# The opening rows of a decoder trunk: norm weights spread by TensorE, the root on ScalarE, two weight splits on GpSimd, orders fixed

## The chip, the cores and the metric

The kernel runs on one core of a Trainium2 chip. A core has five engines that run side by side: TensorE (PE in the profile, with its weight loads as PEld), VectorE (DVE), ScalarE (ACT), GpSimd (POOL) and SyncE (SP, which here only issues transfers). The metric is the device time of one execution in microseconds (us); lower is better.

## The reference

One layer of a decoder trunk on 1024 tokens of width 1024: a root-mean-square norm, eight input projections that feed two token mixers, an output projection, then a second norm and a squared-ReLU MLP, then a last norm. What matters here is the beginning:

```python
def rms_norm(x, gain):
    xf = x.astype(jnp.float32)
    y = xf * lax.rsqrt(jnp.mean(xf * xf, axis=-1, keepdims=True) + NORM_EPS)
    return (y * gain.astype(jnp.float32)).astype(x.dtype)
...
    h = rms_norm(x, norm_mix[l])
...
    proj = h @ w_in
    xa, ga, q, f, v, g, m_a, m_b = jnp.split(proj, SPLIT_POINTS, axis=-1)
```

## The kernel before, in words

The tokens are worked in two halves (c = 0 and 1) of 512, the width in four pairs (p) of 256 channels. All large products are made of three products of numbers in a shorter format: each float32 operand is split into a high part (H, a cast on ScalarE, L82) and a low part (L, the difference of the two, on VectorE, L83), and `mm3` (L119 to L123) multiplies H by L, H by H and L by H. Weights arrive as tiles of 128 x 1024 (`raw`, four buffers) and are split into `wH` and `wL` (six buffers, so three tiles at a time).

The opening is `first_norm(0)` followed by the first `project_v`. `first_norm(0)` issues, all on SyncE's queue, four blocks of 128 rows of x, the norm weights (`gain`, one row of 1024 that the transfer repeats on 128 partitions) and the first three weight tiles. `norm_rows` (L140) then takes a block's mean square (Square with an accumulator, ScalarE), adds epsilon (VectorE), raises to the power -0.5 (GpSimd), and scales the rows by that and by the gain in one VectorE instruction. `transposed` (L147) turns the block into columns by TensorE, in two halves of four 128 x 128 transposes (`xT`), and splits them into `hT0H` and `hT0L`. `project_v` makes `v` (`pv`, one PSUM bank per block of rows, accumulated over four weight tiles): with `by_rows` it takes the first three tiles block by block, then the fourth tile for all blocks. After it come the projections `xa` (`pj_xa`, whose first product ends the opening), `q` and `f`, the gate products `pr` and `pi` of the recurrence, and the rest of the first pair.

What sets the order: a scheduler places the instructions by its own estimate of their times. Only instructions that pass through `keep` while `in_order[0]` is true (that is, until the end of `first_norm(0)`) stay in the order in which the program states them; splits of weights carry a higher priority (`tc.high_priority(400)`). Each engine runs its own list strictly in order. The small tables `pvt`, `mf` and `mu` come on SyncE's queue behind the opening's transfers; `parameters` derives per-channel constants from `pvt` on VectorE and ScalarE.

Of the kernel before, what the change touches and what calls it, by code (L numbers as in the profile page):

```python
# [18 lines left out]
P = 128  # L19
# [23 lines left out]
def trunk(ctx: ExitStack, tc: tile.TileContext, x, wts, mlp, pv, gains, mask_f, mask_u, out):  # L43
# [15 lines left out]
    def bank(tag, name):  # L59
        return ps.tile([P, 512], F32, tag=tag, name=name, bufs={"pj": 4, "sc": 2, "hg": 2}[tag])  # L60
# [16 lines left out]
    def keep(ins):  # L77
        if in_order[0]:
            tc.keep_in_program_order(ins)

    def split(src, h, lo):
        keep(A.copy(h, src))  # L82
        keep(V.tensor_tensor(out=lo, in0=src, in1=h.bitcast(F32), op=ALU.subtract))  # L83

    def raw_tile(name):
        return wp.tile([P, 1024], F32, tag="raw", name=name, bufs=4)
# [1 line left out]
    def load_w(i):  # L88
        raw = raw_tile(f"raw{i}")
        nc.sync.dma_start(raw, wts[i])  # L90
        return raw

    def split_w(i, raw):
        h = wp.tile([P, 1024], F32R, tag="w", name=f"wH{i}", bufs=6)
        lo = wp.tile([P, 1024], F32R, tag="w", name=f"wL{i}", bufs=6)
        with tc.high_priority(400):
            split(raw, h, lo)
        return h, lo

    raws = []  # L100

    def fill_w(n):
        while made[0] < min(n, len(seq)):
            i = seq[made[0]]
            raw = raws.pop(0) if raws else load_w(i)
            ready[made[0]] = split_w(i, raw)
# [8 lines left out]
    def next_w():  # L115
        used[0] += 1
        return get_w(used[0] - 1)

    def mm3(o, ah, al, bh, bl, first, last, goes_on=False):  # L119
        how = {"skip_group_check": True} if goes_on else {}  # L120
# [2 lines left out]
        PE.matmul(o, al, bh, start=False, stop=last, **how)  # L123
# [7 lines left out]
    mhalf = const.tile([P, 8], F32, tag="mhalf", name="mhalf")  # L131
    G.memset(mhalf, -0.5)

    def gain_tile(i, queue=nc.scalar):
        g = const.tile([P, D], F32, tag="gain", name=f"gain{i}", bufs=1)
        queue.dma_start(g, gains[i : i + 1, :].to_broadcast([P, D]))
        return g


    def norm_rows(xt, xn, gain, name):  # L140
        r = const.tile([P, 1], F32, tag="rstd", name=f"rstd_{name}", bufs=4)
        keep(A.activation(xn, xt, AF.Square, scale=D**-0.5, accum_out=r))
        keep(V.tensor_scalar(r, r, EPS, None, op0=ALU.add))  # L143
        keep(G.tensor_tensor(out=r, in0=r, in1=mhalf[:, 0:1], op=ALU.pow))
        keep(V.scalar_tensor_tensor(xn, xt, r[:, 0:1], gain, op0=ALU.mult, op1=ALU.mult))

    def transposed(xn, dst, tt, name):  # L147
        for h in range(2):
            pt = bank("hg", f"xT_{name}_{h}")
            for k in range(4):  # L150
                PE.transpose(pt[:, k * P : (k + 1) * P], xn[:, (4 * h + k) * P : (4 * h + k + 1) * P], ident)
# [14 lines left out]
    def tile_x(name):  # L166
        return xt_pool.tile([P, D], F32, tag="xt", name=name)
# [8 lines left out]
    def mt(tag, name, shape=(P, T), dt=F32, bufs=1):  # L176
        return m.tile(list(shape), dt, tag=tag, name=name, bufs=bufs)
# [60 lines left out]

    X_TAGS = ("g1", "g2", "on", "xc")

    def first_norm(c):
        dst = a2_set(a2h, f"hT{c}")
        xts = []
        for tt in range(4):
            r = c * 4 + tt
            xt = mt(X_TAGS[tt], f"x{r}", (P, D)) if c == 0 else tile_x(f"x{r}")
            nc.sync.dma_start(xt, x[r * P : (r + 1) * P, :])
            xts.append(xt)
            if c == 0 and tt == 0:
                gain0.append(gain_tile(0, nc.sync))  # L250
            if c == 0 and tt < 3:
                raws.append(load_w(seq[tt]))
        xns = {}

        def rows(tt):
            xns[tt] = mt("f" if tt % 2 == 0 else "tmp", f"xn{c}{tt}", (P, D))
            norm_rows(xts[tt], xns[tt], gain0[0], f"x{c}{tt}")

        def weights(n):
            if c == 0:  # L260
                fill_w(n)

        rows(0)
        weights(1)
        transposed(xns[0], dst, 0, f"x{c}0")
        rows(1)
        weights(2)
        for tt in range(1, 4):
            if tt < 3:
                rows(tt + 1)  # L270
            transposed(xns[tt], dst, tt, f"x{c}{tt}")
        weights(3)
        in_order[0] = False
        hT.append(dst)

    def project(c, name):

# [10 lines left out]
    def project_v(c, name, by_rows):  # L288
        v = mt("v", f"v_{name}", (P, 4, 512))
        pp = [bank("pj", f"pv_{name}_{tt}") for tt in range(4)]  # L290
# [8 lines left out]
        early = 3 if by_rows else 0  # L299
        w = [next_w() for _ in range(early)]  # L300
        for tt in range(4):
            for j in range(early):
                product(tt, j, w[j])
        for j in range(early, V_TILES):
# [336 lines left out]

    for c in range(NC):
        if c == 0:
            first_norm(0)
            mu32 = small_inputs()
        else:
            out_proj(0, ys, res0, done0, lambda: first_norm(1))
        ys = a2_set(a2y, f"y{c}")
        for p in range(NPAIR):
            if p % 2 == 0:  # L650
                v = project_v(c, f"{c}{p}", c == 0 and p == 0)
# [417 lines left out]
```

## Time and profile before

| | |
|---|---|
| time, median of 3 runs | 1615.21 us (1615.21 to 1615.22) |
| profiled execution | 1614.85 us |
| its span on the core | 1613.1 us |
| granted TensorE clock, mean | 0.996 |
| busy: PE / DVE / ACT / POOL | 97% / 75% / 47% / 4% |
| first transposes start, first product, first product of pj_xa | 7.76, 10.06, 38.42 us |

Times in the profile are counted from the start of the span. In a row of the timeline stand start, duration, engine, line, operation, and what is written from what; in brackets the idle time of the engine before it and what ended that wait. In a row of waits stand the waiting instruction, the one that it waits for, the total, how often, and the longest. In a row of stretches stand the stretch, its length, then the busy time and the number of instructions of PE, PEld, DVE, ACT and POOL, the granted clock, the share of the transfer engines and GB/s. A row that names a line with three numbers between slashes gives the least, median and greatest duration in ns. A row of transfers ends in KB and in us from issue to landing.

### The profile page before, as it was taken

What the parts mean: (1) busy time and instruction counts of PE and PEld (TensorE: products, weight loads), DVE (VectorE), ACT (ScalarE), POOL (GpSimd) and SP (SyncE); (2) the same over time, 40 slices, a digit from 0 to 9 for tenths busy, and PEclk for the clock granted to TensorE, in tenths of its full rate; (3) what the DMA queues carried; (4) which work ended last, traced back from release to release, by engine and by line L of the source; (5) the groups of instructions that cost most, each with busy time, mean ns of one, the idle gap of its engine ahead of it and who ended that gap; (6) DMA issues with size and microseconds to landing.
All of it is one profiled execution on the core that took longest, in us unless ns stands there. A gap on an engine that the chain in (4) does not pass through costs nothing.

```text
span 1613.1 us, 22407 instructions
## 1 busy us (share of the span) xinstructions
PE 1567.8 (97%) x8856; PEld 1281.7 (79%) x8856; DVE 1209.2 (75%) x1751; ACT 760.2 (47%) x1170; POOL 63.7 (4%) x99
## 2 busy tenths in 40 slices
PE   7999999999999999999999997999999999999997
PEld 6878788787888878788787875888888878888886
DVE  4886954958762877856869688888887888888776
ACT  4544544445442644435444575766777732221113
POOL 0010100100100010000000000000000000000000
PEclk9999999999999999999999998999999999999999
DMA  6222222222244222223222363666666666666652
GB/s 239 92 71 94 86 79 91 81 79 97 80 163 143 93 66 92 79 84 100 67 92 92 118 209 105 248 245 257 242 243 256 223 256 239 256 243 256 247 206 105
DMA packets 57993, 246.46 MB, mean 153 GB/s; under 512 B 6688, under 2 KB 6816, under 8 KB 47136
## 3 DMA queue, kind: packets, MB, share of 16 engines
q1 hardware_dynamic: 56448, 239.79, 41.0%
q10 hardware_dynamic: 1440, 5.24, 1.0%
q8 instruction: 69, 1.13, 0.3%
q14 instruction: 36, 0.29, 0.1%
HBM read 185.24 MB, written 59.77 MB: 152 GB/s over the span
## 4 chain that ended last, share of the span: by engine, by line
PE 79%; DVE 16%; DMA 2%; issue 1%; ACT 1%; POOL 0%; SPq 0%; DVEq 0%; POOLq 0%; ACTq 0%
PE uX L121 3%; PE uX L123 3%; PE uX L122 3%; PE dX L121 3%; PE dX L122 3%; PE dX L123 3%; DVE wL L83 2%; PE pj_ga L123 2%; PE pj_ga L122 2%; PE pj_ga L121 2%; PE pj_ma L121 2%; PE pj_ma L123 2%; PE pj_ma L122 2%; PE pj_f L123 2%; PE pj_f L121 2%; PE pj_f L122 2%
## 5 line engine op out<-in xcount | busy, mean ns | idle before, releaser
L83 DVE TENSOR_TENSOR wL<-raw,wH 128x1024 fp32r<-128x1024 f32 x160 | 194.3, 1215 | 148.3 <-ACT wH L82 145.4
L82 ACT CAST wH<-raw 128x1024 fp32r<-128x1024 f32 x160 | 167.9, 1050 | 182.6 <-issue 51.8
L980 DVE TENSOR_TENSOR acc<-acc,dX 128x512 f32<-128x512 f32 x128 | 86.7, 682 | 27.6 <-PE dX L123 27.4
L82 ACT CAST wA<-q 128x512 fp32r<-128x512 f32 x32 | 19.8, 622 | 129.8 <-PE dX L123 81.9
L980 DVE TENSOR_TENSOR acc<-acc,dY 128x512 f32<-128x512 f32 x64 | 43.4, 683 | 13.8 <-PE dY L123 12.6
L361 DVE RECIPROCAL rr<-rr 128x512 f32<-128x512 f32 x16 | 53.5, 3346 | 0.0
L840 ACT ACTIVATE b<-b 128x512 f32<-128x512 f32 x48 | 30.2, 630 | 37.8 <-DVE b L839 37.8
L327 DVE SCALAR_TENSOR_TENSOR xc<-xp,pvt,xc 128x512 f32<-128x512 f32 x48 | 33.1, 745 | 0.0
L567 ACT ACTIVATE on<-po 128x128 f32<-128x128 f32 x64 | 16.9, 278 | 33.5 <-PE po L557 33.2
L586 ACT ACTIVATE smb<-pj_mb 128x512 f32<-128x512 f32 x16 | 9.6, 597 | 45.2 <-PE pj_mb L123 45.0
L841 ACT ACTIVATE b<-b 128x512 f32<-128x512 f32 x48 | 30.1, 630 | 1.1
L581 ACT ACTIVATE g<-pj_g 128x512 f32<-128x512 f32 x16 | 9.6, 599 | 37.3 <-PE pj_g L123 37.3
L400 DVE TENSOR_TENSOR seg<-seg 128x128 f32<-128x128 f32 (+2 forms) x96 | 26.9, 309 | 0.2
L460 POOL TENSOR_SCALAR seg<-seg 128x128 f32<-128x128 f32 (+1 forms) x16 | 12.6, 788 | 357.7 <-DVE seg L400 357.7
L123 PE MATMUL pj_ga<-hT1H,wL 128*128 128x512 f32 x64 | 26.5, 414 | 0.0
L121 PE MATMUL pv<-wL,hT0H 128*128 128x512 f32 x64 | 26.0, 406 | 0.3 <-DVE wL L83 0.3
L123 PE MATMUL pj_ga<-hT0H,wL 128*128 128x512 f32 x64 | 26.2, 409 | 0.0
L400 DVE TENSOR_TENSOR kk<-kk,seg 128x768 f32<-128x768 f32 (+1 forms) x32 | 26.1, 817 | 0.0
L122 PE MATMUL pj_ga<-hT0H,wH 128*128 128x512 f32 x64 | 25.8, 403 | 0.0
L121 PE MATMUL uX<-h2B11L,wA 128*128 128x512 f32 x64 | 25.0, 391 | 0.7 <-DVE rstd_h L143 0.7
L83 DVE TENSOR_TENSOR wA<-q,wA 128x512 fp32r<-128x512 f32 x32 | 21.9, 685 | 4.9 <-ACT wA L82 4.9
L123 PE MATMUL pv<-wH,hT0L 128*128 128x512 f32 x64 | 25.6, 400 | 0.0
(1854 smaller groups left out, 5167.0 us busy)
## 6 DMA issues: line engine op xcount, KB each, us to landing
raw<-wts_in SPq DMA_DIRECT2D x160, 512.0 KB, 3.3
q<-mlp_in SPq DMA_DIRECT2D x64, 512.0 KB, 3.6
x<-x_in SPq DMA_DIRECT2D x8, 512.0 KB, 6.1
acc<-x ACTq DMA_DIRECT2D x8, 512.0 KB, 5.4
y_out<-acc SPq DMA_DIRECT2D x16, 256.0 KB, 2.0
xs<-x_in SPq DMA_DIRECT2D x8, 256.0 KB, 3.9
x<-xs SPq DMA_DIRECT2D x8, 256.0 KB, 2.0
x2s<-x_in SPq DMA_DIRECT2D x4, 512.0 KB, 5.0
```

Of the source, the lines that this page charges most:

```text
L82: keep(A.copy(h, src))
L83: keep(V.tensor_tensor(out=lo, in0=src, in1=h.bitcast(F32), op=ALU.subtract))
L121: PE.matmul(o, ah, bl, start=first, stop=False, **how)
L122: PE.matmul(o, ah, bh, start=False, stop=False, **how)
L123: PE.matmul(o, al, bh, start=False, stop=last, **how)
L327: V.scalar_tensor_tensor(xc[:, s, :], xp[:, j : j + T], pvt[:, PV_CW + 8 * j + u : PV_CW + 8 * j + u + 1], xc[:, s, :], op0=ALU.mult, op1= ...
L361: V.reciprocal(rec, rec)
L400: mul = lambda o, a, b: V.tensor_tensor(out=o, in0=a, in1=b, op=ALU.mult)
L567: A.activation(on[:, 4 * s + n, :], po[:, n * P : (n + 1) * P], AF.Square, accum_out=ssq[:, 4 * s + n : 4 * s + n + 1])
L840: A.activation(b[:, at, :], b[:, at, :], AF.Relu, scale=-1.0 if at == 2 else 1.0)
L841: A.activation(b[:, at, :], b[:, at, :], AF.Square)
L980: V.tensor_tensor(out=dst, in0=dst, in1=banks[bk, pr], op=op)
```

## The change

The opening becomes a function of its own, `opening()`, and every instruction of it on TensorE, ScalarE, VectorE and GpSimd is kept in program order.

- The norm weights come as one row of 4 KB on ScalarE's queue. TensorE spreads them over the partitions by multiplying a column of ones with the row (two products of plain float32, 512 columns each) into two PSUM banks; VectorE reads them there, in two half-width scalings for each block. ScalarE copies them to SBUF later, for the second half of the tokens.
- Four products of a 128 x 128 tile of ones with itself stand on TensorE ahead of that, and four behind it. Their result is not used.
- The inverse root is Sqrt on ScalarE, with epsilon as its bias, and a reciprocal on VectorE; before, an addition on VectorE and a power on GpSimd. One Sqrt of a single column is run at the start, so the table that ScalarE loads is the one with Sqrt.
- The low parts of the first and the third weight tile are computed on GpSimd.
- SyncE's queue has x0, w0, x1, w1, w2, x2, x3; before it had x0, gain, w0, x1, w1, x2, w2, x3.
- The products of the first three weight tiles are stated block by block: for each tile first the products with its high part, those with its low part later (`product`), the transposes of the next block between them.

```diff
-    def split(src, h, lo):
+    def split(src, h, lo, engine=V):
         keep(A.copy(h, src))
-        keep(V.tensor_tensor(out=lo, in0=src, in1=h.bitcast(F32), op=ALU.subtract))
+        keep(engine.tensor_tensor(out=lo, in0=src, in1=h.bitcast(F32), op=ALU.subtract))
...
+    ones = const.tile([P, P], F32, tag="ones", name="ones")
+    V.memset(ones, 1.0)
+    unit = const.tile([P, 1], F32, tag="unit", name="unit")
+    A.activation(unit, ones[:, 0:1], AF.Sqrt)
...
-                PE.transpose(pt[:, k * P : (k + 1) * P], xn[:, (4 * h + k) * P : (4 * h + k + 1) * P], ident)
+                keep(PE.transpose(pt[:, k * P : (k + 1) * P], xn[:, (4 * h + k) * P : (4 * h + k + 1) * P], ident))
...
+    def opening():
+        dst = a2_set(a2h, "hT0")
+        hT.append(dst)
+        row = mt("seg", "g0row", (P, 1536))[0:1, 0:D]
+        nc.scalar.dma_start(row, gains[0:1, :])
+        xts = [mt(X_TAGS[tt], f"x{tt}", (P, D)) for tt in range(4)]
+        for what in ("x0", "w0", "x1", "w1", "w2", "x2", "x3"):
...
+        def pace(n):
+            for _ in range(n):
+                keep(PE.matmul(warm[:, 0:P], ones, ones, start=True, stop=True))
+
+        pace(4)
...
+        pg = [bank("sc", f"gain_ps{h}") for h in range(2)]
+        for h in range(2):
+            keep(PE.matmul(pg[h], ones[0:1, :], row[:, h * 512 : (h + 1) * 512], start=True, stop=True))
+        pace(4)
...
+        def stats(tt, whole=True):
...
+            keep(A.activation(xns[tt], xts[tt], AF.Square, scale=D**-0.5, accum_out=r))
+            keep(A.activation(r, r, AF.Sqrt, bias=eps_t))
+            if whole:
+                inverse(tt)
+
+        def scaled(tt):
+            for h in range(2):
+                xn, xt = xns[tt][:, halves[h]], xts[tt][:, halves[h]]
+                keep(V.scalar_tensor_tensor(xn, xt, rs[tt][:, 0:1], pg[h], op0=ALU.mult, op1=ALU.mult))
...
+        def product(tt, j, part):
+            for k in (2 * j, 2 * j + 1):
+                hh, hl = (a[:, tt * P : (tt + 1) * P] for a in kt(dst, k))
+                wh, wl = (a[:, k % 2 * 512 : (k % 2 + 1) * 512] for a in w[j])
+                for n, (a, b) in enumerate(((hh, wh), (hl, wh)) if part == "h" else ((hh, wl),)):
+                    keep(PE.matmul(pp[tt], a, b, start=(k, n, part) == (0, 0, "h"), stop=False))
+
+        stats(0)
+        scaled(0)
+        fill_w(1, G)
+        stats(1, False)
+        transposed(xns[0], dst, 0, "x00")
+        fill_w(2)
+        inverse(1)
+        scaled(1)
+        fill_w(3, G)
+        w.extend(next_w(False) for _ in range(3))
+        stats(2)
+        scaled(2)
+        for tt in range(4):
+            for j, part in ((0, "h"), (0, "l"), (1, "h"), (2, "h")):
+                product(tt, j, part)
+            if tt < 3:
+                transposed(xns[tt + 1], dst, tt + 1, f"x0{tt + 1}")
+            if tt == 0:
+                stats(3)
+                scaled(3)
+            for j in (1, 2):
+                product(tt, j, "l")
         in_order[0] = False
-        hT.append(dst)
+        for h in range(2):
+            A.copy(g[:, halves[h]], pg[h])
+        return pp
```

`project_v` then takes over the four banks (`begun`) and adds the fourth weight tile. Outside the opening the orders of the engines differ in the first pair of channels only.

The next rows are ScalarE's list from its first transfer or table load on, before. `xn` is a block's rows (the Square writes there, its sum goes to `rstd_x`), `wH` a weight tile's high part, `hT0H` the high part of a transposed half.

```order
L142 ACT_TABLE_LOAD
L142 ACTIVATE xn_126,rstd_x_127<-x_110 128x1024
L82 CAST wH_132<-raw_114 128x1024
L82 CAST hT0H_106<-xT_x_0_136 128x4x128
L82 CAST hT0H_107<-xT_x_1_143 128x4x128
L142 ACTIVATE xn_150,rstd_x_151<-x_116 128x1024
L82 CAST wH_156<-raw_118 128x1024
L142 ACTIVATE xn_160,rstd_x_161<-x_120 128x1024
```

And now:

```order
L267 DMA g0row<-gains_in 1x1024
L129 ACT_TABLE_LOAD
L129 ACTIVATE unit<-ones 128x1
L298 ACTIVATE xn_148,rstd_x_149<-x_116 128x1024
L299 ACTIVATE rstd_x_149<-rstd_x_149,eps_t 128x1
L82 CAST wH_155<-raw_121 128x1024
L298 ACTIVATE xn_159,rstd_x_160<-x_117 128x1024
L299 ACTIVATE rstd_x_160<-rstd_x_160,eps_t 128x1
L82 CAST hT0H_110<-xT_x_0_163 128x4x128
L82 CAST hT0H_111<-xT_x_1_170 128x4x128
L82 CAST wH_177<-raw_124 128x1024
L82 CAST wH_184<-raw_126 128x1024
```

The Square of the second block now stands ahead of the casts of the first block's transposed halves; the casts of the second and third weight tile stand together right behind them.

TensorE's list up to the first use of the second weight tile, before (`xT` are the transposes, `pv_0` the products of the first block):

```order
L151 MATMUL xT_x_0_136<-ident,xn_126 128x128 x4
L151 MATMUL xT_x_1_143<-ident,xn_126 128x128 x4
L121 MATMUL pv_0_227<-wL_133,hT0H_106 128x512
L122 MATMUL pv_0_227<-wH_132,hT0H_106 128x512
L123 MATMUL pv_0_227<-wH_132,hT0L_108 128x512
```

And now (`warm` takes the products of ones, `gain_ps` the spread norm weights):

```order
L280 MATMUL warm<-ones 128x128 x4
L287 MATMUL gain_ps_136<-g0row,ones 128x512
L287 MATMUL gain_ps_137<-g0row,ones 128x512
L280 MATMUL warm<-ones 128x128 x4
L155 MATMUL xT_x_0_163<-ident,xn_148 128x128 x4
L155 MATMUL xT_x_1_170<-ident,xn_148 128x128 x4
L316 MATMUL pv_0_144<-wH_155,hT0H_110 128x512
L316 MATMUL pv_0_144<-wH_155,hT0L_112 128x512
...
L316 MATMUL pv_0_144<-wL_156,hT0H_110 128x512 x2
L316 MATMUL pv_0_144<-wH_177,hT0H_110 128x512
```

Ten products of float32 stand ahead of the first transposes, and the products with the weights' low part moved behind those with the high part.

VectorE's list around `q` in the first pair, before (`mu` is a mask that is cast once, `q` the first product with the projection `pj_q`, `xcL` the low part of the convolved rows that `pr` needs):

```order
L83 TENSOR_TENSOR xcL_467<-xc_449,xcH_466 128x1024
L225 TENSOR_SCALAR par<-par 128x8
L655 CAST mu<-mu_220 128x1792
L317 COPY xp_1278<-xcar 128x3
L317 COPY xp_1286<-xcar 128x3
L381 TENSOR_TENSOR q_532<-sq_533,pj_q_0_470 128x256x2
```

And now:

```order
L445 TENSOR_TENSOR q_556<-sq_557,pj_q_0_494 128x256x2
L226 TENSOR_TENSOR par<-par 128x8
L228 SCALAR_TENSOR_TENSOR par<-par 128x8
L83 TENSOR_TENSOR wL_567<-raw_564,wH_566 128x1024
L229 TENSOR_SCALAR par<-par 128x8
L719 CAST mu<-mu_320 128x1792
L445 TENSOR_TENSOR q_556<-sq_557,pj_q_1_495 128x256x2
```

The cast of `mu` moved from ahead of both products of `q` to between them.

More of the change, by code (lines that the diff above doesn't have):

```diff
@@ L91, in load_w, with split_w @@
         return raw
-    def split_w(i, raw):
+    def split_w(i, raw, engine=V):
         h = wp.tile([P, 1024], F32R, tag="w", name=f"wH{i}", bufs=6)
@@ L96, in split_w, with fill_w @@
         with tc.high_priority(400):
-            split(raw, h, lo)
+            split(raw, h, lo, engine)
         return h, lo
     raws = []
-    def fill_w(n):
+    def fill_w(n, engine=V):
         while made[0] < min(n, len(seq)):
@@ L105, in fill_w @@
             raw = raws.pop(0) if raws else load_w(i)
-            ready[made[0]] = split_w(i, raw)
+            ready[made[0]] = split_w(i, raw, engine)
             made[0] += 1
@@ L239, in trunk, with first_norm @@
     X_TAGS = ("g1", "g2", "on", "xc")
-    def first_norm(c):
-        dst = a2_set(a2h, f"hT{c}")
-        xts = []
+    def first_norm():
+        dst = a2_set(a2h, "hT1")
+        xts = [tile_x(f"x{4 + tt}") for tt in range(4)]
         for tt in range(4):
[L245 to L252, printed above, removed]
+            nc.sync.dma_start(xts[tt], x[(4 + tt) * P : (5 + tt) * P, :])
@@ L253, in first_norm @@
         xns = {}
         def rows(tt):
[L256 to L261, printed above, removed]
-        rows(0)
[L264 to L268, printed above, removed]
+            xns[tt] = mt("f" if tt % 2 == 0 else "tmp", f"xn1{tt}", (P, D))
+            norm_rows(xts[tt], xns[tt], gain0[0], f"x1{tt}")
@@ L297, in product @@
                 mm3(pp[tt], hh[:, cut], hl[:, cut], w[0][:, cols], w[1][:, cols], k == 0, k == 7)
[L299 to L304, printed above, removed]
+        for j in range(3 if begun else 0, V_TILES):
             w = next_w()
@@ L650, in trunk @@
             if p % 2 == 0:
-                v = project_v(c, f"{c}{p}", c == 0 and p == 0)
+                v = project_v(c, f"{c}{p}", begun if c == 0 and p == 0 else None)
             px = project(c, f"xa{c}{p}")
```

37 lines of the change are left out of this document (27 added, 10 removed).

## The prediction

> **What bounds the kernel now.** The page first: TensorE is busy for 97% of the span, so only time in which it waits or runs slowly can be saved. The waits of TensorE, longest first, say where that is; its first product, the first product of the next stage and the moment at which its pace changes come from the timeline.
>
> ```profile
> PE 1567.8 (97%) x8856; PEld 1281.7 (79%) x8856; DVE 1209.2 (75%) x1751; ACT 760.2 (47%) x1170; POOL 63.7 (4%) x99
> PE xT_x L151 <- DVE xn L145: 8.5, 2, 7.8
> PE xT_h L721 <- DVE rstd_h L143: 5.8, 2, 5.3
> 10.06 0.77 PE L121 MATMUL pv<-wL,hT0H 128*128 128x512 f32 x1 [0.33 <-DVE wL L83]
> 11.90 0.63 PE L122 MATMUL pv<-wH,hT0H 128*128 128x512 f32 x1
> 12.33 0.63 PE L123 MATMUL pv<-wH,hT0L 128*128 128x512 f32 x1
> 13.68 1.06 PE L151 MATMUL xT_x<-ident,xn 128*128 128x128 f32 x8 [0.72 <-DVE xn L145]
> 34.57 0.39 PE L122 MATMUL pv<-wH,hT0H 128*128 128x512 f32 x1
> 37.97 0.39 PE L122 MATMUL pv<-wH,hT0H 128*128 128x512 f32 x1
> 38.42 0.39 PE L121 MATMUL pj_xa<-hT0L,wH 128*128 128x512 f32 x1
> ```
>
> The longest single wait is the opening's: 7.8 us until the first normalised rows exist. The change ends where pj_xa starts, at 38.42. Between the first product (10.06) and there lie 28.36 us. In them TensorE has 96 products to issue, 0.227 us apart at full pace (the 15 from 34.57 to 37.97 take 3.40), 21.8 us, and 24 transposes in three lots of 1.04 (the row at 13.68 to the next product), 3.1 us. What is left, 3.5 us, is loss. Of it 6 x 0.20 = 1.2 us is slow pace: the six products from 10.06 to 12.76 start 0.43 apart (11.90, 12.33). The other 2.3 us are waits, the 0.72 at 13.68 among them.
>
> **The chain to the first product**, by the timeline, the issues with their time to landing, and the end of the kernel for the operations that the opening does not have yet:
>
> ```profile
> 3.99 1.06 ACT L142 ACTIVATE xn<-x 128x1024 f32<-128x1024 f32 x1 [2.00 <-DMA x<-x_in]
> 4.95 0.19 ACT L142 ACTIVATION_READ_ACCUMULATOR xn<-x 128x1 f32 x1
> 5.48 0.56 POOL L144 TENSOR_TENSOR rstd_x<-rstd_x,mhalf 128x1 f32<-128x1 f32 x1 [3.17 <-DVE rstd_x L143]
> 6.42 1.28 DVE L145 SCALAR_TENSOR_TENSOR xn<-x,rstd_x,gain 128x1024 f32<-128x1024 f32 x1 [1.09 <-DMA gain<-gains_in]
> 7.61 1.05 ACT L82 CAST wH<-raw 128x1024 fp32r<-128x1024 f32 x1 [2.47 <-DMA raw<-wts_in]
> 7.76 1.97 PE L151 MATMUL xT_x<-ident,xn 128*128 128x128 f32 x8 [7.76 <-DVE xn L145]
> 8.91 0.59 ACT L82 CAST hT0H<-xT_x 128x512 fp32r<-128x512 f32 x1 [0.25 <-PE xT_x L151]
> 9.83 1.28 DVE L83 TENSOR_TENSOR hT0L<-xT_x,hT0H 128x512 fp32r<-128x512 f32 x2
> 0.72 0.38 SPq L247 DMA_DIRECT2D x<-x_in  x1
> x<-x_in SPq DMA_DIRECT2D x1, 512.0 KB, 3.2
> 1.16 0.42 SPq L136 DMA_DIRECT2D gain<-gains_in  x1
> gain<-gains_in SPq DMA_DIRECT2D x1, 512.0 KB, 5.1
> 1.63 0.42 SPq L90 DMA_DIRECT2D raw<-wts_in  x1
> raw<-wts_in SPq DMA_DIRECT2D x1, 512.0 KB, 6.0
> 2.09 0.43 SPq L247 DMA_DIRECT2D x<-x_in  x1
> x<-x_in SPq DMA_DIRECT2D x1, 512.0 KB, 6.8
> y_out<-acc SPq DMA_DIRECT2D x16, 256.0 KB, 2.0
> L944 ACT ACTIVATE ossq<-ossq,eps_t x8: 280/294/297, 1585.2 to 1607.5; 128x1 f32<-128x1 f32 x8
> 1605.96 1.42 DVE L948 SCALAR_TENSOR_TENSOR acc<-acc,ossq,gain 128x512 f32<-128x512 f32 x2
> 110.18 1.06 PE L547 MATMUL pkv<-v,kT 128*128 128x128 f32 x8
> L547 PE MATMUL pkv<-v,kT x112: 275/275/377, 110.2 to 898.9; 128*128 128x128 f32 x112
> ```
>
> *Transfers.* Issue plus time to landing: x0 3.9, gain 6.3, first weight tile 7.6, x1 8.9. The broadcast gain takes 2.3 us of the queue, the others 1.3 each. Removed from the queue, and its 4 KB row sent by ScalarE's, it lets the weight land at 5.2, x1 at 6.6, then 1.3 us each: w1 7.9, w2 9.2, x2 10.5, x3 11.8. If a second place in the queue costs 2.3 whatever stands there, all of these are 1.0 later.
>
> *Norm of rows 0.* The sum is there at 5.14. Before, add, power and hops reach 6.04, then the gain is waited for until 6.42. Now Sqrt 0.29 and a reciprocal of 0.15 lead to 5.7; two half-width scalings, 0.67 apart as at L948, end at 6.3 and 7.1 if the gain is in PSUM.
>
> *Gain by TensorE.* A plain float32 product leaves two records (112 for the 56 that L547 issues), 0.113 apart, so 128 columns cost 0.23 at full pace and, by 0.43 to 0.23, 0.43 slow; 512 columns cost 0.9 and 1.7. The ones start at about 1.0 (a memset of VectorE stands first) and end at 2.7. The row needs at most the 2.0 us of a y_out block, so lands by 2.8 to 3.0. The gain is done at 4.9 and 6.5, the second four products of ones at 7.4, or 8.1 if the pace is still slow. So the second scaling waits 0.1 and ends at 7.2, the transposes run 7.4 to 8.4. When the pace rises: before, work began at 7.76 (eight transposes in 1.97) and the pace changed between 12.76 and 13.68 (eight in 1.06), 5.0 to 5.9 later. From 1.0 that is 6.0 to 6.9; I take 6.5.
>
> The Trainium skill, TensorE: Matmul & The Clock Gate, Part 1, says that the clock doubles after one busy window of about 3.4 us and that the window runs freely; the trace agrees (0.43 and 0.23), and by that page the pace would rise anywhere from 4.4 to 7.8 us, an estimate.
>
> *ScalarE before the first product* is in a fixed order: Sqrt ends 5.5, weight cast 5.5 to 6.5, Square and Sqrt of x1 6.6 to 8.1, then the transposed halves, 8.1 to 8.7 and to 9.3. The first product is at 8.7, against 10.06: **-1.35**. The price of the order is in it: Square of x1 stands ahead of the cast, and if x1 lands 1.0 later, so does everything after.
>
> *From the first product to pj_xa.* The second product needs hT0L (0.64) at 9.4: wait 0.45. Four more lead to 10.5. ScalarE casts w1 9.3 to 10.3 and w2 to 11.4; eight products end at 12.35. VectorE splits w1 10.35 to 11.55 and scales x1 11.7 to 13.05: the second half of the transposes waits 0.3. Two products with w1's low part and two with w2's take TensorE to 14.75. VectorE scales x2 before it takes the low part of x1 (Sqrt of x2 at 12.9, scaling to 14.6, low part to 15.2): wait 0.45. After that nothing is late: rows 2 and 3 are scaled by 14.6 and 17.4, their transposes needed at 18.2 and 23.2. The waits are 1.2 instead of 2.3, the slow pace (1.2) falls away before the first product: **-2.3**. pj_xa starts at 8.7 + 21.8 + 3.1 + 1.2 = 34.8, not 38.42: -3.6. The fourth weight tile still follows the release of the first by 12 products, 2.7 us, as before, against 2.4 for cast and split.
>
> **GpSimd's two splits** are the price that the trace lacks. VectorE needs 1.22 for the shape. Rows of GpSimd:
>
> ```profile
> L234 POOL MEMSET scT<- x1: 951/951/951, 1.0 to 1.0; 128x1024 f32 x1
> L482 POOL TENSOR_SCALAR scT<-dd x32: 397/416/742, 102.5 to 888.3; 32x256 f32<-32x256 f32 x32
> L460 POOL TENSOR_SCALAR seg<-seg 128x128 f32<-128x128 f32 x8 | 10.7, 1332 | 313.3 <-DVE seg L400 313.3
> 51.35 1.23 DVE L83 TENSOR_TENSOR wL<-raw,wH 128x1024 fp32r<-128x1024 f32 x1
> 49.55 0.19 POOL L336 COPY xcar<-xp 128x3 f32<-128x3 f32 x1 [30.98 <-ACT xp L318]
> 51.57 1.06 POOL L336 COPY xcar<-xp 128x3 f32<-128x3 f32 x1 [1.83 <-ACT xp L318]
> ```
>
> Low end: the same columns only written, 0.95. High end: 128 strided columns in 1.33, times 8, 10.7. Nearest is the contiguous one-input 256 columns in 0.42: four times that is 1.7, and a second input at most doubles it, 3.3. I take 2.5. The first split then runs 6.55 to 9.05, needed at 10.1; the second 11.5 to 14.0, needed at 14.1. So a little over 3 it costs nothing; above 3.4 each us costs two, since the second queues behind the first. The copy of three columns that took 0.19 and, under VectorE's split, 1.06 shows the two engines blocking each other; only w1's split (until 11.55) meets GpSimd's second, for 0.1.
>
> The Trainium skill, GPSIMD Engine Reference, Performance versus the Vector engine, speaks against the move: two-input elementwise work belongs on VectorE, 2293 ns there and 4497 on GpSimd for 2048 columns. Halved, that is an estimate of 2.25 us, with which the sum stays as it is; no run here shows it yet.
>
> **What stays or is hidden.** The table load now serves Sqrt and still ends before x0. Two copies of the gain to SBUF (0.59 each) sit on ScalarE at 16, where nothing waits. Behind pj_xa the order differs in the first pair alone, above all: mu's cast (2.0 us, VectorE) no longer stands ahead of q's first product.
>
> ```profile
> 62.23 0.47 PE L121 MATMUL pr<-xcL,wH 128*128 128x512 f32 x1 [0.76 <-DVE q L381]
> 25.00:30.00 5.00, 5.00 (x23) 4.13 (x22) 0.00 (x0) 0.00 (x0) 0.00 (x0) 1.00 0.32 108
> 90.00:100.00 10.00, 9.35 (x161) 7.21 (x160) 10.00 (x25) 1.99 (x3) 1.04 (x2) 1.00 0.16 54
> ```
>
> That wait of 0.76 can go; the next limit is VectorE, which works through all of 90 to 100 (its 10.00 of 10.00 us) but itself first waits for what pr feeds. Between 0 and -0.8 (to +0.5 if another wait grows); I take **-0.4**.
>
> Sum: -3.6 - 0.4 = -4.0. The profiled execution, 1614.85 (span 1613.1 and 1.75 around it), becomes 1610.85; the median of the runs lies 0.36 above it, 1615.21, so 1611.2.
>
> **Rivals.** (a) The weight and x1 land 1.0 us later than I take it, or the row is late (each us after 3.5 costs near one) and the pace rises late (at 8.0: +0.6): -2.4 to -3.0, 1612.2 to 1612.8. For it: the first two landings are 2.3 apart. Against: the other gaps are 1.3, and only the broadcast differs. (b) GpSimd's split takes 4 to 5 us: +1.2 to +3.2 by the price above, 1612.4 to 1614.4. (c) Slower: the same split as slow as L460. The second one then lands in the middle of the second row block, TensorE idles for twice the excess, and the sum is at zero from 5.4 us, 3.2 us slower from 7.0, and 10.6 us slower at 10.7 (1625.8). Against: L460 has strides of three and four elements, the splits have none. (d) The change does not reach the end: VectorE, full in the first pair, keeps its own times. Then 1613 to 1615. Against: VectorE does nothing from 25 to 30, ahead of the first pair; it has slack to start as early as TensorE lets it.
>
> **Chances.** Forecast 0.56; (a) 0.20; (b) 0.11; (c) 0.05; (d) 0.08. 0.2% of this kernel, about what a measurement can tell, is 3.2 us: the border is 1612.0. The forecast's cases lie from 1610.0 to 1612.2 and a few beyond the border are balanced by those of (a) ahead of it: faster 0.56, same 0.39, slower 0.05. The range takes in (a) and most of (b) and (d), 1610.0 to 1614.4.
>
> **What would show it.** Right: first product near 8.7 with neighbours 0.23 apart, pj_xa near 34.8, GpSimd's splits under 3.4 us, no wait of pr for q. Wrong: a wait of the first products for GpSimd's wL, products of ones that run past 8, casts that stand behind a Square waiting for x1, or TensorE waits in the first pair that grew by what the opening saved.

## The result: slower by half a per cent, and the profile after

| | before | after |
|---|---|---|
| time, median of 6 runs each | 1615.22 us (1613.19 to 1615.85) | 1623.11 us (1622.09 to 1624.82) |
| profiled execution, its span | 1614.85, 1613.1 us | 1622.09, 1620.3 us |
| first product, first product of pj_xa | 10.06, 38.42 us | 10.35, 36.46 us |
| first product of the MLP (uX), last product of the kernel | 980.06, 1604.73 us | 978.58, 1611.95 us |

The ratio is 1.0054 with a 95% interval of 1.0043 to 1.0065. The opening did become shorter, by 1.96 us where 3.6 were forecast. The loss is elsewhere: TensorE reaches the MLP 1.5 us earlier than before and leaves it 7.2 us later.

The page's totals of the changed kernel show it first. TensorE is busy 19.4 us longer than before (1567.8 in the prediction's first row), with 20 records more, which the opening explains.

```profile
PE 1587.2 (98%) x8876; PEld 1286.6 (79%) x8876; DVE 1210.5 (75%) x1754; ACT 763.3 (47%) x1177; POOL 67.6 (4%) x97
```

The products of ones and of the row bring 7.9 us (2.07, 3.78 and 2.08 in the timeline below), though the opening as a whole is only 5.8 us busier, its other products reaching the full pace sooner. The larger part arises in the MLP, the second part of the kernel: there TensorE is busy for 630.1 us instead of 617.4, with 2696 records in both. One stretch of 100 us in the MLP, before and then after (columns as in the prediction's rows of stretches):

```profile
1100.00:1200.00 100.00, 100.00 (x440) 82.04 (x439) 80.78 (x101) 71.13 (x101) 0.00 (x0) 1.00 0.63 246
```

```profile
1100.00:1200.00 100.00, 100.00 (x430) 80.16 (x429) 78.84 (x98) 69.14 (x98) 0.00 (x0) 1.00 0.62 238
```

TensorE never waits in either, the granted clock is full in both, and yet it does 430 products instead of 440. The timeline inside that stretch, before and after, the same products:

```profile
1100.10 0.39 PE L121 MATMUL uX<-h2T4L,wA125H 128*128 128x512 f32 x1
1100.33 0.39 PE L122 MATMUL uX<-h2T4H,wA125H 128*128 128x512 f32 x1
1100.56 0.39 PE L123 MATMUL uX<-h2T4H,wA125L 128*128 128x512 f32 x1
```

```profile
1100.13 0.40 PE L123 MATMUL uX<-h2T4H,wA125L 128*128 128x512 f32 x1
1100.36 0.40 PE L121 MATMUL uX<-h2T4L,wA125H 128*128 128x512 f32 x1
1100.59 0.40 PE L122 MATMUL uX<-h2T4H,wA125H 128*128 128x512 f32 x1
1100.83 0.40 PE L123 MATMUL uX<-h2T4H,wA125L 128*128 128x512 f32 x1
```

Over the whole stage the products start 0.233 us apart in its first half (uX, uY, uZ) and 0.231 to 0.232 in its second (dX, dY, dZ), before 0.227 in both. In the mixer (120 to 900 us) the median is 0.227 in both kernels. The diff does not touch the MLP.

What it does touch is where things lie. `ones` takes 512 bytes of each partition and `unit` 32. Both are constant tiles and stand ahead of nearly everything on the lower side of SBUF, so the lower tiles move, most by 544 bytes and all by 32 modulo 256. The tiles of the upper side stay: their place is set by a spacer ahead of the MLP (`pad.tile([P, 56], F32, ...)`, 224 bytes). By the addresses in the compiled programs, a weight tile and the operand that it is multiplied with (wA125H and h2T4H) were equal modulo 256 bytes before, and are 32 apart after.

The opening in the timeline of the changed kernel:

```profile
1.03 2.07 PE L280 MATMUL warm<-ones 128*128 128x128 f32 x8 [1.03 <-DVE ones L127]
3.04 3.78 PE L287 MATMUL gain_ps<-g0row,ones 1*128 1x512 f32 x4
4.37 1.06 ACT L298 ACTIVATE xn<-x 128x1024 f32<-128x1024 f32 x1 [1.61 <-DMA x<-x_in]
6.20 1.41 DVE L306 SCALAR_TENSOR_TENSOR xn<-x,rstd_x,gain_ps 128x512 f32<-128x512 f32 x2
6.75 2.08 PE L280 MATMUL warm<-ones 128*128 128x128 f32 x8
6.93 2.37 POOL L83 TENSOR_TENSOR wL<-raw,wH 128x1024 fp32r<-128x1024 f32 x1 [4.61 <-ACT wH L82]
7.54 1.06 ACT L298 ACTIVATE xn<-x 128x1024 f32<-128x1024 f32 x1 [0.70 <-DMA x<-x_in]
8.61 1.72 PE L155 MATMUL xT_x<-ident,xn 128*128 128x128 f32 x8
10.35 0.51 PE L316 MATMUL pv<-wH,hT0H 128*128 128x512 f32 x1
11.08 0.50 PE L316 MATMUL pv<-wH,hT0L 128*128 128x512 f32 x1 [0.22 <-DVE hT0L L83]
```

The scaled rows are there at 7.61, but the second lot of ones runs from 6.75 to 8.83 at the slow pace (0.52 per product), and the transposes queue behind it. The full clock is recorded from 10.01 on.

### The profile page after: what moved, and what is told of

The parts are those of the page before. It is cut to its first block, busy times and chain, and to the rows that moved or that the text cites. A ratio compares the mean times of both kernels' runs of the same rounds, so it can differ in the third digit from the quotient of the medians.

```text
span 1620.3 us, 22462 instructions
## 1 busy us (share of the span) xinstructions
PE 1587.2 (98%) x8876; PEld 1286.6 (79%) x8876; DVE 1210.5 (75%) x1754; ACT 763.3 (47%) x1177; POOL 67.6 (4%) x97
## 4 chain that ended last, share of the span: by engine, by line
PE 83%; DVE 14%; issue 1%; ACT 1%; DMA 0%; POOL 0%; DVEq 0%; POOLq 0%; SPq 0%; ACTq 0%
PE dX L121 4%; PE dX L123 4%; PE dX L122 4%; PE uX L121 3%; PE uX L123 3%; PE uX L122 3%; DVE wL L83 2%; PE pj_ga L123 2%; PE pj_ga L122 2%; PE pj_ga L121 2%; PE pj_xa L122 2%; PE pj_ma L123 2%; PE pj_xa L121 2%; PE pj_ma L121 2%; PE pj_ma L122 2%; PE dY L123 2%
## 5 line engine op out<-in xcount | busy, mean ns | idle before, releaser
L123 PE MATMUL pj_ga<-hT1H,wL 128*128 128x512 f32 x64 | 26.5, 414 | 0.0
L121 PE MATMUL uX<-h2B11L,wA 128*128 128x512 f32 x64 | 26.2, 409 | 0.3 <-DVE h2B11L L83 0.3
L123 PE MATMUL pj_ga<-hT0H,wL 128*128 128x512 f32 x64 | 26.2, 409 | 0.0
L122 PE MATMUL uX<-h2B11H,wA 128*128 128x512 f32 x64 | 25.9, 404 | 0.0
L123 PE MATMUL uX<-h2B11H,wA 128*128 128x512 f32 x64 | 25.8, 403 | 0.0
L122 PE MATMUL pj_mb<-hT0H,wH 128*128 128x512 f32 x64 | 25.7, 401 | 0.0
L122 PE MATMUL pj_ga<-hT0H,wH 128*128 128x512 f32 x64 | 25.6, 401 | 0.0
```

The source lines that it names most:

```text
L121: PE.matmul(o, ah, bl, start=first, stop=False, **how)
L122: PE.matmul(o, ah, bh, start=False, stop=False, **how)
```

## The experiments

The kernel before was run on the same chip beside each, and all ratios are against it.

**1. The same placement again.** The changed kernel with the spacer 32 bytes shorter, which moves the upper side by the 32 bytes that the lower side has moved:

```diff
-    pad.tile([P, 56], F32, tag="pad", name="pad")
+    pad.tile([P, 48], F32, tag="pad", name="pad")
```

> The changed kernel with the spacer above the MLP's left operands' partners cut from 56 to 48 floats, so that tiles at the top of SBUF move up by 32 bytes and lie again at the same offset modulo 512 bytes as those at the bottom; no instruction changes. Placement theory (the two new constant tiles, 544 bytes, moved the lower tiles against the upper ones, and a product whose two operands differ there runs at 0.233 us instead of 0.227): the products of the MLP are 0.227 apart again and the time is 1613.0 to 1614.6, 1 to 2 us under before. Timing theory (the shifted opening brings the MLP's transfers or splits into another phase against TensorE): no change from the 1623 of the changed kernel. Absolute theory (lower tiles must lie on multiples of 64 bytes, which they do not in the changed kernel): no change either, 1623.

1610.89 us (9 runs), ratio 0.9979 [0.9969, 0.9990]. The MLP is back at its pace, with nothing else changed:

```profile
1100.00:1200.00 100.00, 100.00 (x440) 82.15 (x439) 80.75 (x100) 71.50 (x101) 0.00 (x0) 1.00 0.63 244
```

So the placement is the whole of the loss, and it is the distance between the two sides that counts: the lower tiles still stand where the changed kernel put them.

**2. The placement alone.** The kernel before with an unused constant tile, in five sizes; nothing of the opening changes.

```diff
+    const.tile([P, 1], F32, tag="spare", name="spare")
```

One number takes 32 bytes:

> The kernel before with one unused constant tile of a single float per partition, which takes 32 bytes and moves every tile above it by as much; the instructions and their order are those of before. Placement theory: the MLP's products 0.232 to 0.234 apart as in the changed kernel, 1623 to 1625 (8 to 10 us slower than before). Timing theory: same as before, 1615.2 within 0.1%. Absolute theory: 8 to 10 us slower too, and the mixer's products perhaps slower as well.

64 numbers, 256 bytes:

> The kernel before with one unused constant tile of 256 bytes. Placement theory: tells the period. If 64, 128 or 256 bytes: same as before, 1615.2. If 512 bytes or more: slower, up to 8 to 10 us. Timing theory: same as before.

128 numbers, 512 bytes:

> The kernel before with one unused constant tile of 512 bytes. Placement theory with a period of 512 bytes or a divisor of it: the MLP's products stay at 0.227 and the time at 1615.2 within 0.1%. If the period is 1024 bytes or more: some us slower, up to the 8 to 10 of the changed kernel. Timing theory: same as before.

Then 16 numbers, 64 bytes:

> The kernel before with an unused constant tile of 64 bytes per partition (16 numbers), which moves every tile on the lower side of SBUF by 64 bytes against those on the upper side. Theory A, the two operands of a product are read without loss when their addresses are equal modulo 64 (or 32 is the only bad half): products of the MLP 0.227 us apart, time within 0.2% of before. Theory B, the period is 128 or 256 bytes: products 0.231 to 0.235 apart and the time 5 to 12 us above before, as with the 32 bytes.

And 32 numbers, 128 bytes:

> The kernel before with an unused constant tile of 128 bytes per partition: all tiles of the lower side move by 128 bytes against those of the upper side. 32 and 64 bytes made the MLP products slow (0.231 to 0.235 us apart, +11 us), 256 and 512 did not. Theory A, the period is 128 bytes: products 0.227 apart, time within 0.2% of before. Theory B, it is 256 bytes: products 0.231 to 0.235 apart, +5 to +12 us.

The same stretch of the MLP in the five, from 32 bytes to 512:

```profile
1100.00:1200.00 100.00, 100.00 (x429) 80.16 (x428) 77.28 (x95) 69.28 (x98) 0.00 (x0) 1.00 0.63 240
```

```profile
1100.00:1200.00 100.00, 100.00 (x429) 80.14 (x429) 77.30 (x96) 69.11 (x97) 0.00 (x0) 1.00 0.63 240
```

```profile
1100.00:1200.00 100.00, 100.00 (x431) 80.43 (x430) 77.61 (x96) 68.96 (x97) 0.00 (x0) 1.00 0.63 241
```

```profile
1100.00:1200.00 100.00, 100.00 (x441) 82.06 (x440) 80.11 (x100) 71.31 (x101) 0.00 (x0) 1.00 0.63 244
```

```profile
1100.00:1200.00 100.00, 100.00 (x440) 82.12 (x439) 80.25 (x100) 71.33 (x101) 0.00 (x0) 1.00 0.63 243
```

| unused tile | ratio | median |
|---|---|---|
| 32 bytes | 1.0067 [1.0050, 1.0084] | 1625.78 us |
| 64 bytes | 1.0067 [1.0051, 1.0083] | 1625.90 us |
| 128 bytes | 1.0062 [1.0048, 1.0076] | 1624.38 us |
| 256 bytes | 0.9996 [0.9987, 1.0005] | 1614.16 us |
| 512 bytes | 0.9995 [0.9986, 1.0005] | 1614.10 us |

An empty tile of 32 bytes costs 0.7%. Of the five distances only the multiples of 256 bytes cost nothing.

**3. Between which accesses.** In the first half of the MLP the moving operand (h2) lies on the upper side, the weights mostly on the lower. Two kernels, made from the one before, separate TensorE's own reads from what else goes on. In the first, a 32-byte tile stands in the first of the pools that hold h2. It moves four of the seven operands, B11, B21, n2 and t1, and nothing else:

```diff
     h2p = [opened(f"h2{i}", side="right") for i in range(4)]
+    h2p[0][0].tile([P, 8], F32, tag="spare", name="spare")
```

> The kernel before with an unused 32-byte tile in the first of the four pools that hold the operands h2 of the MLP's first stage (uX, uY, uZ). It moves the tiles B11, B21, n2 and t1 by 32 bytes against everything else; B22, T3 and T4 and all other tiles of the kernel stay where they are. Only TensorE reads these tiles in that stage. Theory A, the loss arises between TensorE's own reads (the moving operand of a product and the weights that are loaded beside it): products with B11, B21, n2 or t1 are 0.231 to 0.235 us apart, those with B22, T3 or T4 and all of the second stage (dX, dY, dZ) stay at 0.227; +4 to +6 us. Theory B, the loss is TensorE's reads against what the other engines and the transfers do on the two sides: the first stage stays at 0.227 throughout, or all of it is slowed alike.

The timeline of this kernel, in one weight tile's run of products and the next; B21 has been moved, B22 has not:

```profile
1095.21 0.40 PE L121 MATMUL uZ<-h2B21L,wA125H 128*128 128x512 f32 x1
1095.44 0.40 PE L122 MATMUL uZ<-h2B21H,wA125H 128*128 128x512 f32 x1
1095.68 0.40 PE L123 MATMUL uZ<-h2B21H,wA125L 128*128 128x512 f32 x1
1095.91 0.40 PE L121 MATMUL uZ<-h2B21L,wA125H 128*128 128x512 f32 x1
...
1099.35 0.39 PE L121 MATMUL uY<-h2B22L,ws35H 128*128 128x512 f32 x1
1099.58 0.39 PE L122 MATMUL uY<-h2B22H,ws35H 128*128 128x512 f32 x1
1099.81 0.39 PE L123 MATMUL uY<-h2B22H,ws35L 128*128 128x512 f32 x1
1100.03 0.39 PE L121 MATMUL uY<-h2B22L,ws35H 128*128 128x512 f32 x1
```

Three products take 0.70 us with B21 and 0.68 with B22. Over the stage the medians are 0.2335 to 0.235 for the four moved operands, 192 products each, and 0.227 for T3, T4, B22 and for all of the second half. The other kernel has 32 unused bytes ahead of the four landing buffers of the weights (`raw`) and 224 behind them, so these alone stand at another distance:

```diff
     def split_w(i, raw):
+        if not load_w_first:
+            load_w_first.append(wp.tile([P, 56], F32, tag="spare1", name="spare1"))
         h = wp.tile([P, 1024], F32R, tag="w", name=f"wH{i}", bufs=6)
...
     raws = []
+    wp.tile([P, 8], F32, tag="spare", name="spare")
+    load_w_first = []
```

> The kernel before with 32 unused bytes ahead of the four buffers in which weights land (raw) and 224 behind them: only raw and the small tiles' neighbours keep another place, all other tiles of the lower side move by 256 bytes, which cost nothing as an unused tile. TensorE never reads raw; transfers write it, ScalarE and VectorE read it. Theory A (TensorE's own reads): all products of the MLP 0.227 us apart, time within 0.2% of before. Theory B (transfers and the splits that read raw collide with TensorE's reads): products 0.231 to 0.235 apart, +5 to +12 us.

Ratio 0.9995 [0.9986, 1.0005], all medians of the MLP 0.227. So theory A of both holds: the loss arises between TensorE's own two reads, the moving operand and the weights loaded beside it. One rival is left by these two kernels: ScalarE, VectorE and the transfers also touch tiles on the lower side other than `raw`. The trace of the first kernel answers it. Between 1010 and 1270 us the products with moved operands start 0.233 to 0.234 us apart on average also where ScalarE is idle (118 of them), where VectorE is idle (14) and where no transfer is under way (214).

The whole time of the first kernel fell short of what was expected. 768 products at +0.0066 on average are 5.1 us, but the ratio is 1.0010 [1.0001, 1.0020], and the profiled span, of the slowest of its ten executions, is 3.7 longer. In that execution the first half of the MLP takes 6.6 us longer than before (317.8 against 311.2) and the second half 3.5 less (310.0 against 313.5), though its products are 0.227 apart in both. Why the second half is shorter stays open.

One thing is left over. In the changed kernel the second half of the MLP is slow too (0.231 to 0.232), though most of its products have both operands on one side. Its weights and operands alternate between the sides every three products, so the reads of neighbours could meet. That this is the cause is not shown: on average all three products of such a run start late (0.232, 0.230 and 0.233 for L121, L122 and L123), and not only the last, whose neighbour lies on the other side.

**4. The second lot of ones.** From here on the edits start from the changed kernel with the short spacer (first product 10.35, pj_xa 36.67); the ratios are still against the kernel before. Removed is the second lot:

```diff
             keep(PE.matmul(pg[h], ones[0:1, :], row[:, h * 512 : (h + 1) * 512], start=True, stop=True))
-        pace(4)
```

> After with the spacer at 48 numbers (first product at 10.35 us, first product of pj_xa at 36.67), without the second lot of four ones products (4 us wide at most, 6.75 to 8.83 there). Theory A, that lot only stands in the way: the transposes start when the second half-width scaling ends, about 7.65 instead of 8.62, the rise of the granted clock keeps its place (10.0 to 11.3), the first product comes at about 9.5 and pj_xa 0.5 to 0.9 earlier, 35.8 to 36.2. Theory B, the lot is what makes the clock rise when it does: without it the rise moves to 12.5 or later, six or more products at 0.43 us eat up what the earlier transposes bring, and pj_xa stays within 0.3 of 36.67 or comes later. The whole time stays within 1 us of the kernel with the spacer alone.

```profile
7.03 1.94 PE L155 MATMUL xT_x<-ident,xn 128*128 128x128 f32 x8 [0.21 <-DVE xn L305]
8.96 0.79 PE L315 MATMUL pv<-wH,hT0H 128*128 128x512 f32 x1
35.09 0.39 PE L121 MATMUL pj_xa<-hT0L,wH 128*128 128x512 f32 x1
```

Theory A, and by more than it said: transposes and pj_xa 1.6 us earlier, the full clock from 10.80 on, not later. The ratio, 0.9989 [0.9978, 0.9999], does not tell this kernel from the one of experiment 1; 1.6 us is 0.1%.

**5. The splits back on VectorE.**

```diff
-        fill_w(1, G)
+        fill_w(1)
...
-        fill_w(3, G)
+        fill_w(3)
```

> After with the spacer at 48 numbers, the low parts of the first and third weight tile on VectorE (1.22 us each there) instead of GpSimd (2.36 and 2.48). Theory of the prediction: on GpSimd they cost nothing and relieve VectorE; back on VectorE the first one stands between the scaling of x0 and the low parts of the transposed rows, ends at about 8.9 and delays nothing yet (low part of the first half at 10.33), the third tile's stands behind the scaling of x1 and delays low part or scaling of x2 by up to 1.2: pj_xa 0 to 1.2 later than 36.67. Rival: the two engines block each other so much that moving them to GpSimd brought nothing, pj_xa at 36.7 or earlier.

```profile
18.18 0.50 PE L316 MATMUL pv<-wH,hT0L 128*128 128x512 f32 x1 [1.15 <-DVE hT0L L83]
37.79 0.39 PE L121 MATMUL pj_xa<-hT0L,wH 128*128 128x512 f32 x1
```

pj_xa is 1.12 later, by one wait of TensorE for a low part that stands behind the third tile's split on VectorE: the theory of the prediction. The ratio is 0.9984 [0.9975, 0.9994].

**6. What counts as work for the clock.** Four kernels. First the row spread by a full product, in a zeroed tile of 128 rows:

```diff
-        row = mt("seg", "g0row", (P, 1536))[0:1, 0:D]
-        nc.scalar.dma_start(row, gains[0:1, :])
+        row = mt("seg", "g0row", (P, 1536))[:, 0:D]
+        V.memset(row, 0.0)
+        nc.scalar.dma_start(row[0:1, :], gains[0:1, :])
...
-        pace(4)
+        pace(6)
...
-            keep(PE.matmul(pg[h], ones[0:1, :], row[:, h * 512 : (h + 1) * 512], start=True, stop=True))
+            keep(PE.matmul(pg[h], ones, row[:, h * 512 : (h + 1) * 512], start=True, stop=True))
```

> After with the spacer at 48 numbers; the row of norm weights stands in a tile of 128 rows that is zeroed first, and TensorE spreads it with all 128 rows of ones (same result), behind six ones products instead of four. Theory A, a product with one row of 128 does not count as work for the clock: with full products from 1.0 us on, the granted clock rises at 5 to 8 us, the second lot of ones and the transposes run at full pace (0.23 and 0.113 apart), and the first product comes at 9 to 9.7 although the row lands up to 1 us later. Theory B, it counts like any other, and the clock rises when it does for another reason: the rise stays at 10 to 11.3, the first product at 10.35 or, with the later row, up to 1 us later.

This kernel did not separate the theories: the transfer, behind the zeroing, left at 2.09 instead of 0.71, after the first three large ones, and its row was there at 6.67 instead of before 3.04. TensorE stood idle for 2.70 us, the first product came at 13.38 and pj_xa at 39.32, so the times that they gave could not be judged. The ratio is 0.9992 [0.9982, 1.0003]. Next, no products of ones at all, experiment 4 without the first lot too:

```diff
-        pace(4)
         g = const.tile([P, D], F32, tag="gain", name="gain0", bufs=1)
```

> After with the spacer at 48 numbers and without any ones products (the second lot alone removed: transposes at 7.03 us, first product 8.96, first product of pj_xa 35.09, rise of the clock 10.8, span 1609.1). Theory A, the first lot (1.03 to 3.11) is too short and too early to matter, since the row is multiplied from 3.04 to 6.82 behind it and the clock rises 3.3 to 5.6 us after the transposes or later full products begin: first product of pj_xa within 0.3 of 35.09, rise at 10.3 to 12.6. Theory B, the first lot is part of what makes the clock rise: the rise comes one step of 3.41 us later, 14.2, about ten more products run at 0.43 instead of 0.23 and pj_xa starts 1 to 2 us later, 36 to 37.

The full clock came at 13.84 and pj_xa at 36.55, as theory B said. The ratio, 0.9986 [0.9977, 0.9995], is that of experiment 4 within its interval. Then sixteen products of ones in one lot ahead of the row, none behind:

```diff
-        pace(4)
+        pace(16)
         g = const.tile([P, D], F32, tag="gain", name="gain0", bufs=1)
```

> After with the spacer at 48 numbers, sixteen ones products in one lot from 1.03 us ahead of the row's products, none behind them: TensorE then does full products without a gap for 6 to 8 us. Theory A, full products count from the first and products with one row of 128 do not: the clock rises at 4.4 to 7.9 us (one to two steps of 3.41 after 1.03), so the ones end at 6 to 8, the row's products take 1.9 instead of 3.78 if the clock stays up, transposes at 8.5 to 10.5 and all products at 0.23. Theory B, the rise depends on something else than the products ahead (the start of the execution, the total work): it stays at 10 to 12.6, the ones end at 9.3, the row's products at 12 to 13, and pj_xa starts 5 to 6 us later than 35.09.

```profile
1.04 5.51 PE L280 MATMUL warm<-ones 128*128 128x128 f32 x32 [1.04 <-DVE ones L127]
6.48 1.98 PE L287 MATMUL gain_ps<-g0row,ones 1*128 1x512 f32 x4
36.08 0.39 PE L121 MATMUL pj_xa<-hT0L,wH 128*128 128x512 f32 x1
```

Theory A: the full clock from 4.57 on, and the row's products take 1.98 instead of 3.78. The gain is ready only at 8.46, though, so pj_xa starts at 36.08; the ratio is 0.9994 [0.9986, 1.0003]. Last, no ones and the row's two products stated four times:

```diff
-        for h in range(2):
+        for h in (0, 1) * 4:
             keep(PE.matmul(pg[h], ones[0:1, :], row[:, h * 512 : (h + 1) * 512], start=True, stop=True))
```

> After with the spacer at 48 numbers, no ones products, and the two products that spread the row stated four times over (same result): TensorE multiplies one row of 128 without a gap from about 2.3 us. Theory A, a product with one row of 128 does not count as work for the clock: the eight run at the slow pace all through (0.94 per record, 1.88 per product, to about 17.4 us), and the clock rises 3.3 to 6.9 us after the transposes that follow, at 21 to 25 us. Theory B, it counts like any other: the clock rises 3.4 to 6.9 us after 2.3, at 5.7 to 9.2, the later ones take 0.9 to 1.0, the eight end at 10 to 13, and the first products of the projection are 0.23 apart. The whole time is 4 to 12 us above the kernel without ones either way, since the norm waits for the row.

```profile
2.22 13.99 PE L286 MATMUL gain_ps<-g0row,ones 1*128 1x512 f32 x16 [2.22 <-DMA g0row<-gains_in]
16.14 2.03 PE L155 MATMUL xT_x<-ident,xn 128*128 128x128 f32 x8
...
19.25 0.63 PE L314 MATMUL pv<-wH,hT0H 128*128 128x512 f32 x1
19.68 0.53 PE L314 MATMUL pv<-wH,hT0L 128*128 128x512 f32 x1
...
20.50 0.39 PE L314 MATMUL pv<-wH,hT0H 128*128 128x512 f32 x1
20.73 0.39 PE L314 MATMUL pv<-wH,hT0L 128*128 128x512 f32 x1
```

TensorE is busy without a gap for 14 us and never leaves the slow pace: 0.87 for each of the 16 records. The pace changes 3.8 us after the first full products, the transposes (full clock recorded from 19.96). The ratio is 1.0034 [1.0018, 1.0050]. The same count for others, from the first full products after which TensorE goes on with such products to the full clock:

| kernel | full products from | full clock from | apart |
|---|---|---|---|
| before | 7.76 | 12.94 | 5.2 |
| unused tile of 512 / 128 bytes | 7.88 / 7.75 | 11.32 / 14.05 | 3.4 / 6.3 |
| after | 6.75 | 10.01 | 3.3 |
| experiment 4 | 7.03 | 10.80 | 3.8 |
| no ones | 6.99 | 13.84 | 6.9 |
| sixteen ones | 1.04 | 4.57 | 3.5 |
| eight row products | 16.14 | 19.96 | 3.8 |

The clock records of these traces change in steps of 3.41 us (the first stretch at the full clock after the change is 962.56 us long, 282 steps). The Trainium skill, TensorE: Matmul & The Clock Gate, Part 1, says that the clock rises after one busy window of about 3.4 us, and that the windows run freely. By that page the rise would come 3.4 to 6.8 us after the start, an estimate, and the table agrees within 0.2 us (3.3 to 6.9; the other eight traces lie between, 3.4 to 5.7).

Counted back from the rise in such steps, all sixteen traces have full products in 82 to 100% of the last step. The step before it has them in at most 71%, with one exception. Steps filled by the row's products alone bring no rise: one in the changed kernel (3.18 to 6.59) and three in the kernel with eight row products. The kernel with the zeroed row bears on this after all. Of the last step there (8.88 to 12.30) the row's products with all 128 rows take the first 39%; had they not counted, it would have been filled to 61%. So 512 columns do count when all rows are used. The exception is the kernel without ones: its step from 7.01 to 10.42 was filled to 87% and brought no rise, with one wait of 0.43 us in it. Whether that wait or the missing first lot made its clock late stays open; one execution does not settle it.

## Why the prediction was wrong

**The failed step.** The part "What stays or is hidden" has no term for the two new constant tiles. They were costed at nothing by not being named, and no rival stands for a change that alters the pace of products far from it. The 544 bytes cost 11.4 us: the changed kernel is 7.9 above its before, with the distance restored it is 3.5 below (1610.89 against 1614.39). Nothing in the trace of before priced it, but the spacer of 224 bytes ahead of the MLP, without any other use, was in the code and asked the question.

**With the placement restored, the total is near the forecast, but partly by luck.** Experiment 1 took 1610.89 us, 3.5 below its own before (1.6 to 5.0 by its interval), against a forecast of 1611.2 and -4.0. The two terms of the sum do not give that. In its trace pj_xa starts 1.75 earlier and the first pair takes 0.6 longer, -1.1 together. The other 2.4 us are none of the terms. Experiment 5 says so too: there the two terms cancel (-0.63 and +0.6), and the ratio is still 0.9984. Where this part comes from stays open. In the profiled executions of the kernels whose products are 0.227 apart throughout, the MLP takes 621.8 to 625.4 us, 624.7 of them before and 623.4 in experiment 1. Term by term:

- *First product, 8.7 forecast, 10.35 measured.* x0 landed 0.4 later (Square at 4.37, not 3.99). The rest is the second lot of ones: it was to end at 7.4 or 8.1 and ended at 8.83, because the pace did not rise at 6.5. That figure was counted from 1.0, where the products of ones begin; the row's products, 3.04 to 6.82, do not count (experiment 6), and the clock's time began again at 6.75. Without the lot the first product is at 8.96.
- *From the first product to pj_xa, 26.1 forecast:* 36.46 - 10.35 = 26.1. The order of waits was other than told (VectorE's low part 0.22 instead of 0.45, a few products still slow), the sum the same.
- *pj_xa:* -1.96 instead of -3.6, all of the difference ahead of the first product. Experiment 4 gives -3.3. Of rival (a) the late clock came true, at more than its price (10.01, priced at 8.0). Late data did too, but cost little: 0.4 by x0, and x1's Square came at 7.54 instead of 6.6 and delayed nothing, since ScalarE then waited 0.69 for the transposes.
- *GpSimd, 2.5 us taken:* 2.37 and 2.49, nothing waited for them, and back on VectorE they cost 1.1. Rivals (b) and (c) fall. The Trainium skill's page GPSIMD Engine Reference, Performance versus the Vector engine, gave an estimate of 2.25; the measured times are 5 to 11% above it.
- *The first pair, -0.4:* pr no longer waits (0.76 before), but other waits take its place. The waits of TensorE from 34 to 136 us, after:

```profile
PE sc L474 <- DVE seg L464: 0.9, 1, 0.9
PE sc L474 <- DVE q L464: 0.9, 1, 0.9
PE pi L121 <- DVE q L445: 0.5, 1, 0.5
```

They sum to 2.3, before to 1.9, and from pj_xa to the next pair's pj_xa it is 97.16 us instead of 96.52: +0.6, just beyond the worse end given (+0.5). Rival (d) falls: in experiments 1, 4 and 5 pj_xa starts 1.75, 3.33 and 0.63 earlier than before, and the stretch after it is 97.1 each time. What the opening saves arrives at the next pair, less a constant 0.6 for the new order.
- *The range and the chances.* A price of 0.05 for slower was far too low. It came from one mechanism, a slow GpSimd.

## What to carry to other kernels

When a change adds or drops a tile, compare the addresses of the tiles that TensorE multiplies with each other before and after, and restore their distance (here with a spacer) before judging the change itself. If all products of a stage that the diff does not touch are a few per cent further apart, with no wait and a full clock, look at placement first. And filler products only stand in the way when the work behind them is ready: time them to end before the real rows come.

## What was not expected of the hardware

- When the two tiles that TensorE reads for one product are 32, 64 or 128 bytes apart modulo 256, each product of 512 columns starts 0.005 to 0.008 us later (medians 0.232 to 0.235 instead of 0.227), 2 to 4%; with 0 there is no loss.
- Products with one row of 128 kept TensorE busy for 14 us and did not raise the granted clock; full products raised it after 3.3 to 6.9 us.
- GpSimd subtracts two contiguous tiles of 1024 columns in 2.36 to 2.49 us, VectorE in 1.22.
